# 128 rows instead of 64 for the mixer's small products, and products of one shape side by side

## The chip, the cores and the metric

The kernel runs on one core of a Trainium2 chip. Its engines work side by side, each through its own list of instructions in order: PE (TensorE) multiplies matrices, DVE (VectorE) and ACT (ScalarE) do elementwise work and reductions, POOL (GpSimd) does a little of that and issues some DMAs, SP issues most DMAs. Matrix products read SBUF and write PSUM. The metric is the device time of one execution in microseconds (us), lower is better. TensorE's clock has two levels here, 1.2 and 2.4 GHz; the profile shows the level as a granted share, 0.5 or 1.0.

## The reference

One layer of a streaming encoder over 256 tokens of width 2048, with 256 memory tokens. The residual x gets four updates, each wrapped in root-mean-square norms:

```python
x = x + 0.5 * post(FFN1(pre(x)))                  # SwiGLU, width 5504
x = x + post((gA * MLA(h) + gB * RWKV7(h)) @ w_o) # h = pre(x), the mixer
x = x + post(XAttn(pre(x), mem))                  # 4 heads of 256
x = x + 0.5 * post(FFN2(pre(x)))
```

The change lies in the mixer, in three places.

- MLA is attention with 8 heads. A head's score is a product over 128 columns without position plus one over 64 columns with a rotary position: `s = q_nope @ k_nope.T + q_rope @ k_r.T`. The rotary key `k_r` is one for all heads.
- RWKV7 makes its decay and its gate `a` by low-rank products: `tanh(dw) @ w_w2` and `da @ w_a2`, both with 64 inputs and 1024 outputs.
- RWKV7 then runs a recurrence over the tokens with a 64 x 64 state for each of 16 heads, `S = S * w + (S a) b^T + v k^T`, and reads `o = S r`.

## The kernel before

Activations are kept with features on the 128 partitions and tokens along the free axis, or the other way round. Weights stream from memory in tiles of 128 x 1024 numbers (512 KB): SP issues the load (`wraw`), ACT rounds it to fp32r (`whi`, line 179), DVE takes the rest (`wlo`, line 180), and PE does three products, high by high, low by high, high by low (lines 197 and 200 in `lin_ch`, 218 to 220 in `lin_tok`). These streams are most of the kernel's time.

The other products of the mixer are plain fp32 products. Each stands as two instructions in the trace (two passes), so four products show as x8. The profile gives the shape of the part of TensorE's array that an instruction uses: 128\*128 for 128 input rows by 128 output columns, 64\*128 for 64 input rows, 64\*64, 128\*64.

- `mla_attend` (line 568) has for each head and each of two query blocks a product with 128 rows (line 582) and one with 64 (line 583). Two heads share one tile of rotated queries `qrT`: the even head on partitions 0 to 63, the odd one on 64 to 127. The rotary key `krT` stands twice, once in each half. The query blocks have 128 and 256 key columns.
- `rw_prep` (line 692) prepares one group of 8 heads; it runs twice. At line 713 it has 4 low-rank products for the decay (rows 0 to 63 of `twa` and `ww`) and then 4 for `a` (rows 64 to 127), each over 256 tokens; ACT turns each into `lw` or `ta` (line 715). Line 720 scales `lw` once all four parts are there, and line 723 sums it along each chunk by a scan with a constant of zeros and ones that comes from memory in `cst`.
- `rw_gram` and `rw_inverse` then build and invert the within-chunk matrices. The inverse is a long row of small DVE instructions with a DMA to memory and back on both sides; PE goes on with `td` loaded back into `G`.
- `rw_chain` (line 841) walks 8 chunks of 32 tokens in order. In a chunk, for four pairs of heads: `po` gets state times inputs (line 848, 128\*128, not in the first chunk) and `G` times values (line 849, 64\*64); ACT copies `po` to `rhs`; PE multiplies by the inverse (line 856, 64\*64); DVE copies that to `uv`; PE makes the state's update `pn` (line 861, 128\*128) and the outputs (line 870, 128\*64); DVE makes the new state.

```python
for p in range(GP):
    if S is not None:
        nc.tensor.matmul(po[:, p, :], self.ar[:, c, p, :], S[:, p, :], ...)
    nc.tensor.matmul(po[:64, p, :], G[64:, c, p, :64], self.uv[64:, c, p, :], ...)
```

The order of each engine's list is fixed before the run by a planner that works with priorities: what stands in `hot()` (the low-rank products, the chain) comes first when its inputs are ready by the planner's reckoning, and the gaps are filled with products of less urgency: the projection of r and k during the attention, `out_a` and the gate products (`gate`, 8 blocks of columns) during the two groups. [...]

Of the kernel before, what the change touches and what calls it, by code (L numbers as in the profile page):

```python
# [10 lines left out]
F32 = mybir.dt.float32  # L11
F32R = mybir.dt.float32r
I32 = mybir.dt.int32
AF = mybir.ActivationFunctionType
ALU = mybir.AluOpType
# [3 lines left out]
P = 128  # L19
D = 2048  # L20
T = 256
# [29 lines left out]
CHUNK = 32  # L51
NC = T // CHUNK
GP = 4
HEADS_G = 2 * GP
# [2 lines left out]
TWO_PI_PARTS = (6.28125, 1.93500518798828125e-3, 2.0 * math.pi - 6.28125 - 1.93500518798828125e-3)  # L57
ROUND_MAGIC = 1.5 * 2.0 ** 23

CST = {"gram": 128, "sel": GP * HEADS_G, "scan": T}  # L60
NCST = sum(CST.values())


def _constants():
    out = {}
    row = np.arange(P)
    x, h, s = row // 64, row // 32 % 2, row % 32
    ok = np.where(x[None, :] == 0, s[:, None] < s[None, :], s[:, None] <= s[None, :])
    out["gram"] = (ok & (h[:, None] == h[None, :])).astype(np.float32)
    head = np.arange(GP)[None, :, None] + GP * (row[:, None, None] // 64)  # L70
    out["sel"] = (head == np.arange(HEADS_G)[None, None, :]).astype(np.float32).reshape(P, -1)
    out["scan"] = np.broadcast_to((np.arange(T) % CHUNK != 0).astype(np.float32), (P, T))
    m = np.zeros((P, 256), np.float32)
    m[:64, 192:] = -1.0e30
    inv = 10000.0 ** (-np.arange(32) / 32.0)
    return np.concatenate([out[n] for n in CST], axis=1), m, np.tile(inv.astype(np.float32), (P, 1))


class Layer:
# [416 lines left out]
    def mla_latents(self, mp, pool, normed):  # L496
        nc, w_in = self.nc, self.a["w_in"]
        h, r, _ = normed
        self.pad(pool, 224)
        self.cqh = pool.tile([P, 4, T], F32R, name="cqh")  # L500
        self.cql = pool.tile([P, 4, T], F32R, name="cql")
        self.ckh = pool.tile([P, 2, T], F32R, name="ckh")
        self.ckl = pool.tile([P, 2, T], F32R, name="ckl")
        self.krT = pool.tile([P, T], F32, name="krT")

        self.lin_tok(w_in, KD, 0, 512, h[:, :, 0], h[:, :, 1],
                     lambda t, ps: self.latent_norm(mp, ps, r, 512, self.cqh, self.cql, "n_q_lat", t))

        def ev(t, ps):
            self.latent_norm(mp, ps[:, :256], r, 256, self.ckh, self.ckl, "n_kv_lat", t)  # L510
            kr = pool.tile([P, 2, 2, 32], F32, tag="kr", name="kr", bufs=2)
            x1, x2 = ps[:, 256:288].unsqueeze(1), ps[:, 288:320].unsqueeze(1)
            self.rope(pool, x1, x2, kr[:, 0:1, 0, :], kr[:, 0:1, 1, :], t)
            nc.vector.tensor_scalar_mul(kr[:, 0], kr[:, 0], r[t])
            nc.vector.tensor_copy(out=kr[:, 1], in_=kr[:, 0])
            pt = self.pst.tile([P, P], F32, tag="tr", name="tr")
            nc.tensor.transpose(pt, kr.rearrange("p a b c -> p (a b c)"), self.ident)
            nc.scalar.copy(out=self.krT[:, t * P : (t + 1) * P], in_=pt)

        self.lin_tok(w_in, KD, 512, 320, h[:, :, 0], h[:, :, 1], ev)  # L520

# [46 lines left out]
    def mla_attend(self, pool):  # L568
        nc = self.nc
        oT = self.hpool.tile([P, 2, 8, T], F32R, tag="big", name="oT")  # L570
        self.oTh, self.oTl = oT[:, 0], oT[:, 1]
        mask = pool.tile([P, 256], F32, name="mask")
        nc.scalar.dma_start(out=mask, in_=self.a["mask"])
        scale = 192.0 ** -0.5
        for h in range(8):
            rp = slice(h % 2 * 64, h % 2 * 64 + 64)
            pt = self.pst.tile([P, 3, P], F32, tag="tr", name="tr")
            for qb in range(NT):
                n = (qb + 1) * P
                s = slice(qb * P, (qb + 1) * P)  # L580
                ps = self.pss.tile([P, 256], F32, tag="sm", name="sc")
                nc.tensor.matmul(ps[:, :n], self.qnT[:, h, s], self.knT[:, h, :n], start=True, stop=False)
                nc.tensor.matmul(ps[:, :n], self.qrT[rp, h // 2, s], self.krT[rp, :n], start=False, stop=True)
                sc = pool.tile([P, 256], F32, tag="sc", name="sc", bufs=2)
                nc.vector.tensor_add(sc[:, :n], ps[:, :n], mask[:, 256 - n :])
                p = self.softmax(pool, sc[:, :n], scale)
                for kb in range(qb + 1):
                    nc.tensor.transpose(pt[:, qb + kb, :], p[:, kb * P : (kb + 1) * P], self.ident)
            pT = pool.tile([P, 3, P], F32, tag="pT", name="pT", bufs=2)
            nc.scalar.copy(out=pT, in_=pt)  # L590
            po = self.pss.tile([P, T], F32, tag="sm", name="po")
            vs = slice(h * P, (h + 1) * P)
            nc.tensor.matmul(po, self.mv[:, 0, vs], pT[:, :2, :].rearrange("p a b -> p (a b)"), start=True, stop=False)
            nc.tensor.matmul(po[:, P:], self.mv[:, 1, vs], pT[:, 2, :], start=False, stop=True)
            self.split(po, self.oTh[:, h, :], self.oTl[:, h, :])
# [44 lines left out]
    def rw_proj_lora(self, pool, normed):  # L640
        h, _, row = normed
        nc = self.nc
        self.twa = pool.tile([P, T], F32, name="twa")
        self.sg = pool.tile([P, T], F32, name="sg")

        def ev(j, ps):
            dst, nm = ((self.twa, "wa"), (self.sg, "g"))[j]
            self.shifted(pool, dst, ps, row, self.col("mu_" + nm, 0), self.col2("omu_" + nm, 0))
            if j == 0:
                nc.scalar.activation(out=dst[:64], in_=dst[:64], func=AF.Tanh)  # L650
            else:
                nc.scalar.activation(out=dst, in_=dst, func=AF.Tanh, scale=0.5)
                nc.vector.tensor_scalar(out=dst, in0=dst, scalar1=0.5, scalar2=0.5, op0=ALU.mult, op1=ALU.add)

        self.lin_ch(self.a["w_in"], KD, 3904, 256, h, ev)
# [36 lines left out]
    def rw_prep(self, pool, g, r, k, bon):  # L692
        nc, a = self.nc, self.a
        p4 = lambda nm: pool.tile([P, GP, T], F32, tag="p4", name=nm, bufs=6)
        ww = pool.tile([P, 512], F32, tag="ww", name="ww")
# [3 lines left out]
        for h in range(2):  # L699
            o = g * 512 + h * 256  # L700
            nc.gpsimd.dma_start(
                out=self.uv[64 + h * 32 : 96 + h * 32].rearrange("s c p v -> s c (p v)"),
                in_=self.vsh[:, o : o + 256].rearrange("(c s) x -> s c x", s=CHUNK))
        nc.gpsimd.memset(self.bk, 0.0)

        lw, ta, kk = p4("lw"), p4("ta"), p4("kk")
        for dst, q, bias in ((lw, slice(0, 64), "hw0"), (ta, slice(64, P), "ha0")):
            for p2 in range(GP // 2):
                ps = self.pss.tile([P, 2, T], F32, tag="sm", name="lora")
                for j in range(2):  # L710
                    p = 2 * p2 + j
                    with self.hot():
                        nc.tensor.matmul(  # L713
                            ps[:, j, :], ww[q, p * P : (p + 1) * P], self.twa[q, :], start=True, stop=True)
                    nc.scalar.activation(
                        out=dst[:, p, :], in_=ps[:, j, :], func=AF.Tanh,
                        bias=self.col2(bias, g * GP + p), scale=0.5)
        for p in range(GP):
            nc.scalar.activation(out=kk[:, p, :], in_=k[:, p, :], func=AF.Copy, scale=self.col("k_k", g * GP + p))
        nc.vector.tensor_scalar(  # L720
            out=lw, in0=lw, scalar1=1.0, scalar2=-0.5 * KAPPA, op0=ALU.add, op1=ALU.mult)
        for p in range(GP):
            nc.vector.tensor_tensor_scan(
                out=lw[:, p, :], data0=self.c("scan"), data1=lw[:, p, :], initial=0.0, op0=ALU.mult, op1=ALU.add)
        sq = p4("sq")
        nc.scalar.activation(out=sq, in_=kk, func=AF.Square)
        sel = self.c("sel").rearrange("p (a b) -> p a b", a=GP)
        ssp = self.pss.tile([P, NT, HEADS_G], F32, tag="sm", name="ssp")
        for t in range(NT):
            for p in range(GP):  # L730
                with self.hot():
                    nc.tensor.matmul(
                        ssp[:, t, :], sq[:, p, t * P : (t + 1) * P], sel[:, p, :],
                        start=(p == 0), stop=(p == GP - 1))
# [3 lines left out]
            out=rt, in0=rt, in1=self.mhalf.unsqueeze(2).broadcast_to([P, NT, HEADS_G]), op=ALU.pow)  # L738
        x = pool.tile([P, NT, GP, P], F32, tag="p4", name="bych", bufs=6)
        for t in range(NT):  # L740
            for h in range(2):
                nc.vector.tensor_copy(
                    out=x[:, t, :, h * 64 : (h + 1) * 64],
                    in_=rt[:, t, h * GP : (h + 1) * GP].unsqueeze(2).broadcast_to([P, GP, 64]))
        for p2 in range(GP // 2):
            ps = self.pss.tile([P, 2, T], F32, tag="sm", name="rnb")
            for j in range(2):
# [5 lines left out]
                out=kk[:, 2 * p2 : 2 * p2 + 2, :], in0=kk[:, 2 * p2 : 2 * p2 + 2, :], scalar=-1.0, in1=ps,  # L753
# [87 lines left out]
    def rw_chain(self, pool, g, G, wc):  # L841
        nc = self.nc
        S = None
        for c in range(NC):
            po = self.pss.tile([P, GP, 64], F32, tag="sm", name="po")
            for p in range(GP):
                if S is not None:
                    nc.tensor.matmul(po[:, p, :], self.ar[:, c, p, :], S[:, p, :], start=(p == 0), stop=False)  # L848
                nc.tensor.matmul(  # L849
                    po[:64, p, :], G[64:, c, p, :64], self.uv[64:, c, p, :],  # L850
                    start=(S is None and p == 0), stop=(p == GP - 1))
# [353 lines left out]
```

## Time and profile before

| | us |
|---|---|
| median of 3 runs (lowest, highest) | 2438.91 (2430.94, 2445.75) |
| the profiled execution | 2441.6 |
| its span, first to last instruction | 2439.8 |

The page gives for each engine the time in which it was busy and, in 40 slices, how this changes. The mixer's attention lies at about 860 to 940 us of the span, the first group's preparation at 940 to 1075, its chain at 1075 to 1132, the second group's preparation at 1126 to 1265 and its chain at 1265 to 1332. In a timeline the first number is the start and the second the duration of an instruction or a merged row of them; passes overlap, so what a row takes from PE is read as the start of the next row less its own start.

### The profile page before, as it was taken

To read this page: it belongs to the slowest core of one execution; us is meant where nothing else is said; L and a number is where in the kernel's file an instruction comes from. 1 tells how busy PE (TensorE), PEld (TensorE's weight loads), DVE (VectorE), ACT (ScalarE), POOL (GpSimd) and SP (SyncE) were. 2 spreads that over 40 slices of the span, in tenths; PEclk is the share of its full clock that TensorE was granted. 3 is DMA by queue.
4 is the path that set the end of the run, shared out by engine and by line. 5 is a ranking of instruction groups with operands and counts; after the bars stand their busy time and mean duration, and the time that the engine had idled before them with its cause. 6 is when DMAs were issued, how large, how long until landed. Compare 5 with 4: busy or idle time off the path is not lost.

```text
span 2439.8 us, 33193 instructions
## 1 busy us (share of the span) xinstructions
PE 2385.9 (98%) x12682; PEld 2021.7 (83%) x12682; DVE 1487.9 (61%) x2262; ACT 1144.7 (47%) x1700; POOL 85.9 (4%) x126
## 2 busy tenths in 40 slices
PE   8999999999999999999999899999999999999997
PEld 6888888878878887887878688987888888888886
DVE  6666666644457576764873856555666666664444
ACT  6444444434446555443432446445544444444443
POOL 0000000000000102002011100000000000000000
PEclk9999999999999999998989999999999999999999
DMA  7555555556665643452553676545455555555654
GB/s 257 190 190 190 190 190 190 187 196 195 198 195 201 233 141 130 156 170 90 181 191 109 206 262 202 178 148 190 157 190 190 190 190 190 190 198 192 204 194 144
DMA packets 138719, 450.36 MB, mean 185 GB/s; under 512 B 24000, under 2 KB 26560, under 8 KB 138304
## 3 DMA queue, kind: packets, MB, share of 16 engines
q1 hardware_dynamic: 132896, 434.17, 53.1%
q0 software_dynamic: 4944, 13.64, 1.9%
q8 instruction: 99, 1.62, 0.3%
q10 hardware_dynamic: 720, 0.44, 0.1%
q14 instruction: 60, 0.49, 0.1%
HBM read 437.69 MB, written 10.49 MB: 184 GB/s over the span
## 4 chain that ended last, share of the span: by engine, by line
PE 91%; DVE 4%; DMA 2%; issue 1%; ACT 1%; POOL 1%; SPq 0%; DVEq 0%; ACTq 0%; POOLq 0%
PE mm L197 30%; PE mm L200 15%; PE mm L219 13%; PE mm L220 13%; PE mm L218 13%; DVE wlo L180 2%; PE po L848 1%; PE po L849 1%; PE gr L803 1%; PE pn L861 1%; ACT whi L179 1%; DMA ov<-osc 0%; PE lora L713 0%; PE po L870 0%; DVE X L387 0%
## 5 line engine op out<-in xcount | busy, mean ns | idle before, releaser
L180 DVE TENSOR_TENSOR wlo<-wraw,whi 128x1024 fp32r<-128x1024 f32 (+2 forms) x796 | 958.2, 1206 | 711.3 <-ACT whi L179 698.4
L179 ACT CAST whi<-wraw 128x1024 fp32r<-128x1024 f32 (+2 forms) x796 | 824.0, 1037 | 902.5 <-PE mm L220 484.2
L197 PE MATMUL mm<-hT,whi 128*128 128x512 f32 x3296 | 1146.9, 394 | 8.9 <-DVE hT L289 6.1
L200 PE MATMUL mm<-hT,wlo 128*128 128x256 f32 x3296 | 912.4, 282 | 1.9 <-DVE wlo L180 1.9
L197 PEld LDWEIGHTS mm<-hT,whi 128*128 128x128 f32 x3296 | 613.6, 188 | 137.8 <-ACT whi L179 7.1
L200 PEld LDWEIGHTS mm<-hT,wlo 128*128 128x128 f32 x3296 | 620.8, 188 | 15.5 <-DVE wlo L180 3.8
L218 PE MATMUL mm<-whi,mh 128*128 128x512 f32 x688 | 267.6, 389 | 1.2 <-ACT whi L179 1.2
L219 PE MATMUL mm<-wlo,mh 128*128 128x512 f32 x688 | 267.8, 389 | 0.5 <-DVE wlo L180 0.5
L220 PE MATMUL mm<-whi,ml 128*128 128x512 f32 x688 | 267.7, 389 | 0.0
L219 PE MATMUL mm<-wlo,hT 128*128 128x512 f32 (+2 forms) x512 | 190.8, 373 | 3.9 <-DVE wlo L180 3.9
L218 PE MATMUL mm<-whi,hT 128*128 128x512 f32 (+2 forms) x512 | 190.3, 373 | 1.9 <-ACT whi L179 1.7
L220 PE MATMUL mm<-whi,hT 128*128 128x512 f32 (+2 forms) x512 | 190.2, 372 | 0.0
L218 PEld LDWEIGHTS mm<-whi,mh 128*128 128x128 f32 x688 | 129.1, 188 | 28.1 <-ACT whi L179 1.5
L219 PEld LDWEIGHTS mm<-wlo,mh 128*128 128x128 f32 x688 | 129.2, 188 | 27.9 <-DVE wlo L180 1.0
L220 PEld LDWEIGHTS mm<-whi,ml 128*128 128x128 f32 x688 | 129.2, 188 | 26.7
L206 ACT COPY half<-mm 128x256 f32<-128x256 f32 x206 | 75.5, 367 | 137.6 <-PE mm L197 137.6
L207 DVE TENSOR_TENSOR half<-half,mm 128x256 f32<-128x256 f32 x206 | 85.6, 417 | 55.0 <-ACT half L206 55.0
L219 PEld LDWEIGHTS mm<-wlo,hT 128*128 128x128 f32 x512 | 99.2, 194 | 20.1 <-DVE wlo L180 5.2
L218 PEld LDWEIGHTS mm<-whi,hT 128*128 128x128 f32 x512 | 99.0, 194 | 17.7 <-ACT whi L179 2.3
L220 PEld LDWEIGHTS mm<-whi,hT 128*128 128x128 f32 x512 | 99.2, 194 | 15.5 <-issue 1.6
L252 POOL TENSOR_TENSOR rstd<-rstd,mhalf 128x1 f32<-128x1 f32 x22 | 12.0, 552 | 1812.5 <-DVE rstd L250 1798.7
L218 PE MATMUL mm<-whi,oT 128*128 128x512 f32 x128 | 51.4, 403 | 1.4 <-ACT whi L179 1.4
(276 smaller groups left out, 1896.5 us busy)
## 6 DMA issues: line engine op xcount, KB each, us to landing
wraw<-in_w_ffn_up SPq DMA_DIRECT2D x172, 512.0 KB, 4.3
wraw<-in_w_ffn_gate SPq DMA_DIRECT2D x171, 512.0 KB, 4.3
wraw<-in_w_ffn_down SPq DMA_DIRECT2D x168, 512.0 KB, 4.2
wraw<-in_w_in SPq DMA_DIRECT2D x124, 512.0 KB, 3.3
wraw<-in_w_o SPq DMA_DIRECT2D x32, 512.0 KB, 4.2
wraw<-in_w_ckv SPq DMA_DIRECT2D x31, 512.0 KB, 3.3
wraw<-in_w_oa SPq DMA_DIRECT2D x16, 512.0 KB, 3.2
wraw<-in_w_ob SPq DMA_DIRECT2D x16, 512.0 KB, 4.5
```

Source lines behind the costliest of these rows:

```text
L179: nc.scalar.copy(out=hi[:, e], in_=raw[:, e])
L180: self.last_split = nc.vector.tensor_sub(out=lo[:, e], in0=raw[:, e], in1=hi[:, e].bitcast(F32))
L197: both = lambda: nc.tensor.matmul(ps[j], hi[:, s], x[:, k], start=(k == 0), stop=(k == nk - 1))
L200: nc.tensor.matmul(ps[j][:, 0, :], lo[:, s], x[:, k, 0], start=False, stop=False)
L206: nc.scalar.copy(out=y, in_=ps[j][:, 1, :])
L207: nc.vector.tensor_add(y, y, ps[j][:, 0, :])
L218: nc.tensor.matmul(ps[t], xh[:, k, s], hi, start=(k == 0), stop=False)
L219: nc.tensor.matmul(ps[t], xh[:, k, s], lo, start=False, stop=False)
L220: self.last_mm = nc.tensor.matmul(ps[t], xl[:, k, s], hi, start=False, stop=(k == nk - 1))
L803: nc.tensor.matmul(ps[:, p, :], self.bk[:, c, p, :], self.ar[:, c, p, :], start=True, stop=True)
L848: nc.tensor.matmul(po[:, p, :], self.ar[:, c, p, :], S[:, p, :], start=(p == 0), stop=False)
L849: nc.tensor.matmul(po[:64, p, :], G[64:, c, p, :64], self.uv[64:, c, p, :], start=(S is None and p == 0), stop=(p == GP - 1))
```

## The change

The sums that are computed stay the same; zeros are added to operands, and one loop is cut in two.

- `krT` becomes two tiles side by side, one with the key in rows 0 to 63 and zeros below, one with zeros above. The product of line 583 then takes all 128 rows of `qrT`: the other head's queries meet zeros. POOL clears the tile, and ACT writes it with two copies for each token block instead of one.
- `twa` likewise becomes two: `tanh(dw)` with zeros below, `da` with zeros above, so that one product of 128 rows and 512 columns gives a decay part and an `a` part. Eight products for a group become four. The shifted projection is first written to `sg`, then moved.
- The scan's constant is not loaded but made by two POOL memsets in each group, in the buffer of `ww`, of which there is one: it waits until the low-rank products have read `ww`, and the load of `ww` for the second group waits for the scans of the first.
- In `rw_chain` all four products of line 848 come before the four of line 849.

```diff
-        self.krT = pool.tile([P, T], F32, name="krT")
+        self.krT = pool.tile([P, 2, T], F32, name="krT")
+        nc.gpsimd.memset(self.krT, 0.0)
...
-            nc.scalar.copy(out=self.krT[:, t * P : (t + 1) * P], in_=pt)
+            for j in range(2):
+                q = slice(j * 64, j * 64 + 64)
+                nc.scalar.copy(out=self.krT[q, j, t * P : (t + 1) * P], in_=pt[q])
...
-                nc.tensor.matmul(ps[:, :n], self.qrT[rp, h // 2, s], self.krT[rp, :n], start=False, stop=True)
+                nc.tensor.matmul(ps[:, :n], self.qrT[:, h // 2, s], self.krT[:, h % 2, :n], start=False, stop=True)
...
-        self.twa = pool.tile([P, T], F32, name="twa")
+        self.twa = pool.tile([P, 2, T], F32, name="twa")
+        nc.gpsimd.memset(self.twa, 0.0)
...
-                nc.scalar.activation(out=dst[:64], in_=dst[:64], func=AF.Tanh)
+                nc.scalar.activation(out=self.twa[:64, 0, :], in_=dst[:64], func=AF.Tanh)
+                nc.scalar.copy(out=self.twa[64:, 1, :], in_=dst[64:])
...
+        for p in range(GP):
+            ps = self.pss.tile([P, 2, T], F32, tag="sm", name="lora")
+            with self.hot():
+                nc.tensor.matmul(ps, ww[:, p * P : (p + 1) * P], self.twa, start=True, stop=True)
+            for j, (dst, bias) in enumerate(((lw, "hw0"), (ta, "ha0"))):
+                nc.scalar.activation(
+                    out=dst[:, p, :], in_=ps[:, j, :], func=AF.Tanh,
+                    bias=self.col2(bias, g * GP + p), scale=0.5)
+        scan = pool.tile([P, NC, CHUNK], F32, tag="ww", name="scan")
+        nc.gpsimd.memset(scan, 1.0)
+        nc.gpsimd.memset(scan[:, :, 0:1], 0.0)
...
             for p in range(GP):
                 if S is not None:
                     nc.tensor.matmul(po[:, p, :], self.ar[:, c, p, :], S[:, p, :], start=(p == 0), stop=False)
+            for p in range(GP):
                 nc.tensor.matmul(
                     po[:64, p, :], G[64:, c, p, :64], self.uv[64:, c, p, :],
```

## Rows read from the trace of the kernel before

**Rows 1.** The page's head, PE's line of part 1 (busy time, share of the span, instructions), and the granted clock in 40 slices of part 2 (tenths of full speed).

```profile
span 2439.8 us, 33193 instructions
PE 2385.9 (98%) x12682; PEld 2021.7 (83%) x12682; DVE 1487.9 (61%) x2262; ACT 1144.7 (47%) x1700; POOL 85.9 (4%) x126
PEclk9999999999999999998989999999999999999999
```

**Rows 2.** The chain that ended last, by engine, from part 4 of the page.

```profile
PE 91%; DVE 4%; DMA 2%; issue 1%; ACT 1%; POOL 1%; SPq 0%; DVEq 0%; ACTq 0%; POOLq 0%
```

**Rows 3.** Busy time by stretch: the stretch, its length, busy us and instructions of PE, PEld, DVE, ACT, POOL, then the granted clock, the DMA engines' share and GB/s. The latents, the attention, the first chain; then three stretches cut at the edges of a fall of the clock.

```profile
770.00:800.00 30.00, 28.68 (x153) 24.16 (x152) 18.88 (x43) 16.67 (x30) 2.75 (x5) 1.00 0.51 179
860.00:940.00 80.00, 78.02 (x412) 60.98 (x412) 54.72 (x151) 42.74 (x90) 4.96 (x4) 1.00 0.35 118
1075.00:1140.00 65.00, 65.00 (x389) 48.36 (x389) 23.09 (x38) 18.64 (x35) 12.61 (x19) 0.90 0.28 92
1123.80:1127.20 3.40, 3.40 (x21) 2.28 (x19) 0.00 (x0) 0.69 (x2) 2.66 (x3) 1.00 0.06 18
1127.20:1144.30 17.10, 17.10 (x51) 10.13 (x50) 4.68 (x7) 9.13 (x17) 2.20 (x4) 0.50 0.23 66
1263.70:1287.60 23.90, 23.27 (x86) 18.10 (x84) 9.73 (x16) 4.42 (x7) 3.79 (x5) 0.50 0.31 99
```

**Rows 4.** What PE waited for between 700 and 1420 us (line, releaser: us in total, times, longest); one row of it.

```profile
PE pu L856 <- DMA G<-td: 3.8, 1, 3.8
```

**Rows 5.** Timeline of PE in a chunk of the first chain: the first two of the eight alternating rows of lines 848 and 849, the gate products behind them, and the next chunk's first row.

```profile
1078.27 0.33 PE L848 MATMUL po<-S,ar 128*128 128x64 f32 x2
1078.54 0.33 PE L849 MATMUL po<-uv,G 64*64 64x64 f32 x2
...
1080.65 0.50 PE L220 MATMUL mm<-whi,hT 128*128 128x512 f32 x1
1080.99 0.39 PE L218 MATMUL mm<-whi,hT 128*128 128x512 f32 x1
1081.22 0.39 PE L219 MATMUL mm<-wlo,hT 128*128 128x512 f32 x1
...
1086.43 0.33 PE L848 MATMUL po<-S,ar 128*128 128x64 f32 x2
```

**Rows 6.** The same chunk's products that stand grouped by shape: four of 64\*64, and four of 128\*128 with 64 columns ahead of four of 128\*64.

```profile
1081.99 0.68 PE L856 MATMUL pu<-rhs,G 64*64 64x64 f32 x8
1082.60 0.50 PE L219 MATMUL mm<-wlo,hT 128*128 128x512 f32 x1
...
1083.63 1.00 PE L861 MATMUL pn<-uv,bk 128*128 128x64 f32 x8
1084.56 0.68 PE L870 MATMUL po<-uv,G 128*64 128x64 f32 x8
```

**Rows 7.** ACT in that chunk, the copy between lines 849 and 856 (in brackets the idle time before it and what ended it).

```profile
1080.76 0.37 ACT L853 COPY rhs<-po 64x256 f32<-64x256 f32 x1 [1.13 <-PE po L849]
```

**Rows 8.** The second chain's second chunk, at the granted clock 0.50: its first row and the gate product behind the eight; then the first row of the third chunk.

```profile
1272.37 0.52 PE L848 MATMUL po<-S,ar 128*128 128x64 f32 x2
...
1276.29 0.79 PE L219 MATMUL mm<-wlo,hT 128*128 128x512 f32 x1
...
1287.14 0.52 PE L848 MATMUL po<-S,ar 128*128 128x64 f32 x2
```

**Rows 9.** Timeline of PE in the attention, around one product of line 583.

```profile
875.65 0.39 PE L582 MATMUL sc<-knT,qnT 128*128 128x128 f32 x2
875.97 0.49 PE L583 MATMUL sc<-krT,qrT 64*128 64x128 f32 x2
876.38 0.50 PE L197 MATMUL mm<-hT,whi 128*128 128x512 f32 x1
876.72 0.28 PE L200 MATMUL mm<-hT,wlo 128*128 128x256 f32 x1
```

**Rows 10.** The low-rank products of the first group: a run of two products between products of `out_a`, and later a run of one.

```profile
944.84 1.13 PE L713 MATMUL lora<-twa,ww 64*128 64x256 f32 x4
945.90 0.51 PE L218 MATMUL mm<-whi,oT 128*128 128x512 f32 x1
946.33 1.13 PE L713 MATMUL lora<-twa,ww 64*128 64x256 f32 x4
...
947.82 0.70 PE L713 MATMUL lora<-twa,ww 64*128 64x256 f32 x2
948.45 0.49 PE L220 MATMUL mm<-whi,oT 128*128 128x512 f32 x1
```

**Rows 11.** The second group's, at the granted clock 0.50: a run of two products (a decay part and an `a` part) and a run of one.

```profile
1132.31 1.23 PE L713 MATMUL lora<-twa,ww 64*128 64x256 f32 x4
1133.47 0.80 PE L218 MATMUL mm<-whi,hT 128*128 128x512 f32 x1
1134.19 1.49 PE L713 MATMUL lora<-twa,ww 64*128 64x256 f32 x4
...
1136.33 1.22 PE L713 MATMUL lora<-twa,ww 64*128 64x256 f32 x2
1137.48 0.79 PE L220 MATMUL mm<-whi,hT 128*128 128x512 f32 x1
```

**Rows 12.** POOL clearing `bk` in the first group.

```profile
940.76 3.53 POOL L704 MEMSET bk<- 128x4096 f32 x1
```

More of the change, by code (lines that the diff above doesn't have):

```diff
@@ L58 @@
 ROUND_MAGIC = 1.5 * 2.0 ** 23
-CST = {"gram": 128, "sel": GP * HEADS_G, "scan": T}
+CST = {"gram": 128, "sel": GP * HEADS_G}
 NCST = sum(CST.values())
@@ L71, in _constants @@
     out["sel"] = (head == np.arange(HEADS_G)[None, None, :]).astype(np.float32).reshape(P, -1)
-    out["scan"] = np.broadcast_to((np.arange(T) % CHUNK != 0).astype(np.float32), (P, T))
     m = np.zeros((P, 256), np.float32)
@@ L575, in mla_attend @@
         for h in range(8):
-            rp = slice(h % 2 * 64, h % 2 * 64 + 64)
             pt = self.pst.tile([P, 3, P], F32, tag="tr", name="tr")
@@ L642, in rw_proj_lora @@
         nc = self.nc
-        self.twa = pool.tile([P, T], F32, name="twa")
+        self.twa = pool.tile([P, 2, T], F32, name="twa")
         self.sg = pool.tile([P, T], F32, name="sg")
+        nc.gpsimd.memset(self.twa, 0.0)
         def ev(j, ps):
-            dst, nm = ((self.twa, "wa"), (self.sg, "g"))[j]
+            dst, nm = self.sg, ("wa", "g")[j]
             self.shifted(pool, dst, ps, row, self.col("mu_" + nm, 0), self.col2("omu_" + nm, 0))
             if j == 0:
-                nc.scalar.activation(out=dst[:64], in_=dst[:64], func=AF.Tanh)
+                nc.scalar.activation(out=self.twa[:64, 0, :], in_=dst[:64], func=AF.Tanh)
+                nc.scalar.copy(out=self.twa[64:, 1, :], in_=dst[64:])
             else:
@@ L706, in rw_prep @@
         lw, ta, kk = p4("lw"), p4("ta"), p4("kk")
[L707 to L717, printed above, removed]
+        for p in range(GP):
[9 more added lines that the diff above has]
+        nc.gpsimd.memset(scan[:, :, 0:1], 0.0)
+        scan = scan.rearrange("q c s -> q (c s)")
         for p in range(GP):
@@ L723, in rw_prep @@
             nc.vector.tensor_tensor_scan(
-                out=lw[:, p, :], data0=self.c("scan"), data1=lw[:, p, :], initial=0.0, op0=ALU.mult, op1=ALU.add)
+                out=lw[:, p, :], data0=scan, data1=lw[:, p, :], initial=0.0, op0=ALU.mult, op1=ALU.add)
         sq = p4("sq")
```

## The prediction

> **What bounds the kernel now.** I read the page first: PE is busy for 98% of the span [rows 1], and the chain that ended last runs through PE for 91% of it [rows 2]. So PE bounds nearly everything, and time that leaves PE's list counts if nothing else becomes late. Then the stretches of the mixer: PE is busy for 78.02 of 80 us in the attention and for 65.00 of 65 in the first chain, where DVE has 23 and ACT 19 [rows 3]. The largest PE wait in the mixer for something other than weights or a norm is 3.8 us, once, for the inverse of the second group coming back by DMA [rows 4].
>
> A busy PE need not be a PE that gets on, so the third view is the timeline, read from start to start. In a chunk of the chain the gate products follow each other every 0.23 us (1080.99 to 1081.22), but the first one after the eight alternating products keeps PE for 0.34 (1080.65 to 1080.99) [rows 5]. The four pairs of lines 848 and 849 take 2.38 us (1078.27 to 1080.65). Products that stand grouped by shape are faster: four of 64\*64 take 0.61 (1081.99 to 1082.60), four of 128\*128 with 64 columns 0.93 (1083.63 to 1084.56), each with the step to the next shape in it [rows 6]. What costs is the step from one shape to another.
>
> The fourth is the clock. Its mean in the first chain's stretch is 0.90: from 1127.20 it is at 0.50 for 17.10 us, with PE busy for all of the 3.40 us before, in which lie the last alternating rows, one low-rank product and few gate products. It is at 0.50 again from 1263.70 for 23.90 us, behind the wait for the inverse [rows 3, 4].
>
> **The change, part by part.** The sum is made against the profiled execution, 2441.6 us (span 2439.8); the median of the runs shown is 2438.9, 2.7 less.
>
> *The chain's grouping.* Lines 848 and 849 keep their counts and shapes. Grouped, they should cost what lines 861 and 856 cost: 0.93 + 0.61 = 1.54 in place of 2.38, so 0.84 less a chunk [rows 5, 6]. The first chunk of a group has no line 848, so 2 x 7 = 14 chunks gain. One stands wholly at the lower clock and takes 3.92 (1272.37 to 1276.29) [rows 8]; its gain lies between 0.84 and the same share of 3.92, 1.38; I take 1.1. Together 13 x 0.84 + 1.1 = 12.0 us. Does a wait take its place? ACT's copy to `rhs` starts at 1080.76, just behind the last 64\*64 product, ends at 1081.13, and line 856 starts at 1081.99 [rows 6, 7]: 0.86 us of slack, filled by gate products, and the change moves the end of line 849 and the copy together.
>
> *The attention's rotary product.* Two passes of 256 columns differ by 0.43 (below), so two of 128 need 0.22. Line 582 ahead of line 583 takes 0.32 (875.65 to 875.97), line 583 itself 0.41, and the weight product behind it 0.34 in place of 0.23 [rows 5, 9]: 0.10 + 0.19 + 0.11 = 0.40 us for one step out and back. All of it goes, since the product with zeros has the shape of its neighbours and the same columns. 16 products give 6.4 us. A gain as small as half of this would need DVE or ACT to set the pace there; they are busy for 55 and 43 of 80 us [rows 3].
>
> *The low-rank products, first group.* A run of two products takes 1.06 (944.84 to 945.90), a run of one 0.63 (947.82 to 948.45): one product is 0.43, and 0.20 of each run is the step. The single weight product between two runs takes 0.43 in place of 0.23 (945.90 to 946.33), so 0.20 more [rows 5, 10]. That is again 0.40 for each run, and 5 runs give 2.0 us. The columns stay: 4 products of 512 columns, 0.86 each as twice 0.43, against 8 of 0.43.
>
> *The second group* has six runs, one at the full clock and five at the lower one. There a run of one takes 1.15 (1136.33 to 1137.48) and a run of two 1.16 (1132.31 to 1133.47): a decay part on rows 0 to 63 and an `a` part on rows 64 to 127 ran at the same time [rows 11]. So the runs hold about 0.63 + 3 x 1.15 + 1.16 + 1.49 = 6.7 us, and four products of 512 columns at that clock would hold 4 x 1.72 = 6.9: no gain inside. The weight product between two runs takes 0.72 (1133.47 to 1134.19) against some 0.45, twice the 0.23 of the full clock, so about 0.3 more [rows 5, 11]; over five runs 5 x 0.3 = 1.5, with the loss of 0.2 and the first run's 0.1 some 1.4 us.
>
> The Trainium skill has a rule that speaks against this part: TensorE: Matmul & The Clock Gate, Part 3 (Packing small matmuls), says that products of few rows in different row groups run at the same time. The trace agrees where the planner happened to put two such side by side [rows 11], and in the first group, where each run held two decay parts or two `a` parts, it shows none [rows 10]. By that rule the eight products of a group, paired, would need 4 x 0.43 instead of the 4 x 0.86 with zeros: 1.7 us a group, or 3.4 in all, that the zeros give away against a packed version, though not against this kernel.
>
> *The clock.* The fall at 1127.20 came behind the place where most steps lay together. With the chain grouped and the low-rank product in the neighbours' shape that place is denser. If the fall stays away, the 17.10 us need about half, so up to 8.5 less, of which 1.4 is counted already: 7 more. If it comes as before, nothing. I take half, 3.5: it comes, but is over sooner, since the five runs within it no longer break the stream.
>
> *What is added.* POOL clears `krT` and `twa` (512 columns each) and makes the scan's constant twice (256 and 8): at 3.53 us for 4096 columns [rows 12] some 1.3 us in all, on an engine that is busy for 86 us of the span [rows 1]. In the second group `lw` is complete after the seventh tanh instead of the fourth, and the scan waits for POOL; what it feeds is needed after the key's norm has gone through PE, POOL and DVE, and PE has gate products meanwhile. I cost it at nothing; without that cover it would be two products and a memset, 2 x 0.86 + 0.23, or 2 us a group. ACT gets three copies of 64 partitions more, 0.37 each by the nearest row [rows 7], two of them in the latents' stretch, where PE lacks 1.3 of 30 us [rows 3]: between 0 and 1.1; I take 1.1, as this is the one place where ACT could be late. POOL's load of the second `ww` now stands behind the first group's scans, long before that group's products use it.
>
> Sum: 12.0 + 6.4 + 2.0 + 1.4 + 3.5 - 1.1 = 24.2 us. 2441.6 - 24.2 = 2417.4; against the median 2438.9 it is 2414.7. I forecast 2415.
>
> **Rivals.**
> - *The clock no longer falls in the chains.* For it: the fall at 1127.20 had no idle PE ahead of it, only steps. Against: the second one stands behind the wait for the inverse, which the change doesn't touch. Both gone would give up to 3.5 + 12 (half of 23.90) more; with the first gone and the second shortened by half, 2415 - 3.5 - 6 = about 2405, at the far end 2400. Chance 0.17.
> - *The gain becomes a wait for the inverse.* PE already waits 3.8 us there [rows 4]; DVE's row of small instructions sets that time. What is saved before the second group's low-rank products moves DVE's start as well, what is saved in and after them (1.4 + 3.5) does not: 2415 + 5 = 2420. If the attention's and the first group's gains (8.4) were held up as well, 2428. Chance 0.14.
> - *The change does not do what it says:* the planner's order changes with the fewer low-rank products, gate products land between the chain's products, and the chain keeps its steps. Then only 6.4 + 2.0 + 1.4 remain, 2429. Against: the chain's instructions are urgent and all ready at once. Chance 0.05.
> - *Slower: the chain runs at the lower clock.* A chunk takes 8.16 us at the full clock (1078.27 to 1086.43) and 14.77 at the lower one (1272.37 to 1287.14) [rows 5, 8], so 6.6 more. Shorter urgent rows could leave PE waiting between them, and a wait stood ahead of the second fall. The gain of 24 is used up from the fourth further chunk; from the sixth the kernel is over 0.5% slower. With seven, one whole chain, 2415 + 46 = 2461. Against: with less dense work the clock was at 0.50 for only two pieces of the chains [rows 3], and each hand-over is filled. Chance 0.06.
>
> **How the numbers follow.** The forecast has 0.58, with its own range 2408 to 2422. Faster by over 0.5%, about what a measurement of this kernel can tell from no change, means under 2426.7: the forecast, the first rival and about half of the second, 0.82. The rest of the second and the third are within 0.5%: 0.12. Slower 0.06. The range reaches from the first rival's 2400 to past the third's 2429, 2432.
>
> **What would show it.** Lines 583 and 713 as 128\*128; the step from 64\*64 to 128\*128 ahead of line 848 gone, and line 848's first row to the end of line 849 taking 1.5 us instead of 2.4; weight products behind lines 583 and 713 at 0.23 us. PE's busy time about 20 us less, with its instructions down by 16. Wrong it would be if 1.5 us show and the span doesn't shrink by 20: then PE's waits, above all for `G<-td`, have grown, or the clock's row shows longer stretches at 0.50.

## The result, and the profile after

The changed kernel takes 2409.56 us (median of 4 runs, 2409.18 to 2411.64) against 2434.93 for the kernel before, run 4 times (2430.35 to 2445.75): ratio 0.9891, 95% interval 0.9854 to 0.9928, 25.4 us less. The forecast was 2415, some 24 less, in a range from 2400 to 2432. The profiled executions are 30.0 us apart, 2441.6 and 2411.64; that of before lay well above its median, at a mean granted clock of 0.986 against 0.992.

The page's head, PE's line and the granted clock of the changed kernel, then its chain by engine, as [rows 1, 2]:

```profile
span 2409.9 us, 33179 instructions
PE 2355.2 (98%) x12666; PEld 2006.5 (83%) x12666; DVE 1487.8 (62%) x2262; ACT 1145.7 (48%) x1703; POOL 87.8 (4%) x132
PEclk9999999999999999999999999999999999999999
PE 90%; DMA 3%; DVE 3%; issue 2%; ACT 1%; POOL 1%; SPq 0%; DVEq 0%; POOLq 0%; ACTq 0%
```

PE's busy time fell by 30.7 us and the span by 29.9, and PE has 16 instructions fewer. DVE, ACT and POOL are busy for the same time as before to within 2 us: nothing but PE's list got shorter, and PE still bounds the kernel. A part of the 30.7 is the clock's: the two eights in its row of [rows 1] are gone.

PE in the first chunk of the first chain that has a state, in the changed kernel (line 849 is now 854, line 856 is 861):

```profile
1074.63 1.00 PE L852 MATMUL po<-S,ar 128*128 128x64 f32 x8
1075.56 0.67 PE L854 MATMUL po<-uv,G 64*64 64x64 f32 x8
1076.16 0.50 PE L219 MATMUL mm<-whi,hT 128*128 128x512 f32 x1
1076.50 0.39 PE L217 MATMUL mm<-whi,hT 128*128 128x512 f32 x1
...
1077.51 0.67 PE L861 MATMUL pu<-rhs,G 64*64 64x64 f32 x8
...
1081.94 1.00 PE L852 MATMUL po<-S,ar 128*128 128x64 f32 x8
```

From 1074.63 to 1076.16 the eight products take 1.53 us, against 2.38 in [rows 5]. The next chunk starts 7.31 later, against 8.16, so the whole 0.85 reaches the chunk's period; line 861 starts 1.35 behind the first gate product (1076.16 to 1077.51), against 1.34 before, without a wait.

The attention, as [rows 9], and the low-rank products of the second group, as [rows 11]:

```profile
876.97 0.39 PE L583 MATMUL sc<-knT,qnT 128*128 128x128 f32 x2
877.19 0.39 PE L584 MATMUL sc<-krT,qrT 128*128 128x128 f32 x2
877.33 0.48 PE L196 MATMUL mm<-hT,whi 128*128 128x512 f32 x1
877.65 0.28 PE L199 MATMUL mm<-hT,wlo 128*128 128x256 f32 x1
...
1118.88 1.02 PE L713 MATMUL lora<-twa,ww 128*128 128x512 f32 x2
1119.83 0.68 PE L875 MATMUL po<-uv,G 128*64 128x64 f32 x8
...
1121.24 1.88 PE L713 MATMUL lora<-twa,ww 128*128 128x512 f32 x4
1122.56 0.80 PE L218 MATMUL mm<-wlo,hT 128*128 128x512 f32 x1
1123.19 0.39 PE L219 MATMUL mm<-whi,hT 128*128 128x512 f32 x1
```

The product ahead of the rotary one (line 582 before, 583 here) takes 0.22 in place of 0.32. From its start to that of the second weight product it is 0.68 us, where [rows 9] have 1.07 (875.65 to 876.72): 0.39 less, one step out and back. Two of the wide low-rank products and the gate product behind them take 1.95 us (1121.24 to 1123.19), which is 2 x 0.86 and 0.23 with no step; one ahead of a 128\*64 row takes 0.95 (1118.88 to 1119.83), so there 0.09 of a step is left.

Five stretches of the changed kernel, columns as in [rows 3]: the attention, the end of the first chain with the low-rank products, the fall of the clock in the second chain, and two short falls, one over the first group's low-rank products and one behind the mixer:

```profile
860.00:940.00 80.00, 76.60 (x433) 64.25 (x432) 58.31 (x162) 44.94 (x94) 8.62 (x6) 1.00 0.43 135
1116.60:1127.60 11.00, 11.00 (x60) 7.32 (x58) 4.77 (x7) 8.96 (x18) 3.84 (x9) 1.00 0.29 82
1244.40:1254.70 10.30, 9.32 (x37) 7.28 (x36) 7.02 (x13) 2.04 (x3) 2.41 (x3) 0.50 0.61 206
940.70:944.10 3.40, 3.30 (x5) 1.51 (x5) 0.00 (x0) 1.21 (x3) 0.00 (x0) 0.51 1.02 265
1483.40:1486.80 3.40, 3.40 (x17) 3.40 (x18) 3.40 (x8) 2.62 (x8) 0.00 (x0) 0.50 0.89 289
```

Two of PE's waits between 700 and 1400 us, as [rows 4]:

```profile
PE pu L861 <- DMA G<-td: 3.3, 1, 3.3
PE lora L713 <- DMA ww<-in_w_a: 2.2, 1, 2.2
```

The stretch that ran at the clock 0.50 for 17.10 us [rows 3] runs at 1.00. The second fall, behind the wait for the inverse, is still there, 10.3 us long in place of 23.90. The wait for the inverse did not grow (3.8 in [rows 4]); a wait for the first group's low-rank weights is new.

### The profile page after: what moved, and what is told of

Its sections match the earlier page's. It is cut to its first block, busy times and chain, and to the rows that moved or that the text cites. A ratio compares the mean times of both kernels' runs of the same rounds, so it can differ in the third digit from the quotient of the medians.

```text
span 2409.9 us, 33179 instructions
## 1 busy us (share of the span) xinstructions
PE 2355.2 (98%) x12666; PEld 2006.5 (83%) x12666; DVE 1487.8 (62%) x2262; ACT 1145.7 (48%) x1703; POOL 87.8 (4%) x132
## 4 chain that ended last, share of the span: by engine, by line
PE 90%; DMA 3%; DVE 3%; issue 2%; ACT 1%; POOL 1%; SPq 0%; DVEq 0%; POOLq 0%; ACTq 0%
PE mm L196 30%; PE mm L199 16%; PE mm L218 13%; PE mm L219 13%; PE mm L217 13%; DVE wlo L179 1%; DMA ov<-osc 1%; PE gr L807 1%; ACT whi L178 1%; DMA wraw<-in_xT 1%; PE pn L866 1%; DVE X L386 1%; PE po L852 0%; PE po L875 0%; PE po L854 0%
## 5 line engine op out<-in xcount | busy, mean ns | idle before, releaser
L217 PE MATMUL mm<-whi,hT 128*128 128x512 f32 (+2 forms) x512 | 187.3, 367 | 2.1 <-ACT whi L178 1.5
L219 PE MATMUL mm<-whi,hT 128*128 128x512 f32 (+2 forms) x512 | 187.9, 368 | 0.0
L206 DVE TENSOR_TENSOR half<-half,mm 128x256 f32<-128x256 f32 x206 | 85.7, 418 | 54.8 <-ACT half L205 54.8
```

Of the source, the lines that this page charges most:

```text
L206: nc.vector.tensor_add(y, y, ps[j][:, 0, :])
L217: nc.tensor.matmul(ps[t], xh[:, k, s], hi, start=(k == 0), stop=False)
L219: self.last_mm = nc.tensor.matmul(ps[t], xl[:, k, s], hi, start=False, stop=(k == nk - 1))
```

## The experiments

The runs of the kernel before scatter over more than 20 us, and with them their mean granted clock, from 0.983 to 0.993. Over the 46 runs of it beside the experiments, a straight line gives 2.0 us for each 0.001 of clock. So each kernel is shown by its median and also by the mean of its runs at 0.992 and 0.993, which compares the work at nearly one clock (called the equal clock below); and by how many runs lay under 0.990. Where a kernel was run twice, its runs are taken together. The runs beside the experiments come from three chips; at the equal clock the kernel before took 2428.5, 2429.3 and 2429.0 us on them. The scatter of the runs leaves a standard error of 0.4 to 1.1 us on each of these means, so a difference of one or two us between them is not clear of noise.

| kernel | medians, us | runs | under 0.990 | at 0.992 and 0.993 (runs) |
|---|---|---|---|---|
| before | 2432.0, 2437.1, 2432.3 | 46 | 16 | 2428.8 (20) |
| grouping alone | 2416.6, 2415.0 | 12 | 0 | 2416.3 (10) |
| rotary product alone | 2426.3 | 12 | 2 | 2423.2 (4) |
| low-rank products alone | 2425.3 | 12 | 2 | 2425.0 (8) |
| all but the grouping | 2417.7, 2419.6 | 12 | 0 | 2419.6 (8) |
| the changed kernel | 2409.6, 2408.1 | 10 | 0 | 2409.5 (7) |
| more alternation | 2419.0 | 7 | 1 | 2419.4 (5) |
| packed low-rank products | 2415.0 | 6 | 0 | 2411.7 (2) |
| low-rank weights first | 2407.9 | 6 | 0 | 2407.2 (2) |

**One part at a time.** Grouping alone is the last piece of the diff put into the kernel before:

```diff
...
                     nc.tensor.matmul(po[:, p, :], self.ar[:, c, p, :], S[:, p, :], start=(p == 0), stop=False)
+            for p in range(GP):
                 nc.tensor.matmul(
...
```

> The kernel before with the grouping of lines 848 and 849 alone. Theory (the price is in the steps between shapes, the clock follows from how dense the work is): the eight products of a chunk take 1.54 us in place of 2.38, 14 chunks give 12 us less; the second clock fall (23.9 us before, 10.2 after) is short here too, which gives up to 6 more; the fall at the end of the first chain may stay, as the low-rank runs are as before. 2417 to 2425. Rival (the low-rank products' steps make both falls): 12 us less and both falls as long as before.

Measured: 2416.59, ratio to the kernel before 0.9924 (0.9900 to 0.9947), just under the range expected; at the equal clock 12.5 us less, against 12.0 by the steps. In its profile the second fall was 10.2 us long and the one at the end of the first chain did not come, though the low-rank runs were as before.

The rotary product alone takes the edits of `krT` and line 583:

```diff
...
-                nc.tensor.matmul(ps[:, :n], self.qrT[rp, h // 2, s], self.krT[rp, :n], start=False, stop=True)
+                nc.tensor.matmul(ps[:, :n], self.qrT[:, h // 2, s], self.krT[:, h % 2, :n], start=False, stop=True)
...
```

> The kernel before with the 128-row rotary product alone. Theory: 16 steps out and back at 0.40 us, 6.4 us less in the attention, of which a part becomes a wait for the first group's low-rank weights behind it: 3 to 6 us less. Rival (the attention is paced by ACT and DVE): under 2 us less, with PE's waits in the attention longer. Clock falls in the chains as before in both.

Measured: 2426.27, ratio 0.9966 (0.9945 to 0.9987), 5.7 us less at the equal clock. In its profile the first to the last score product span 60.6 us, where the kernel before has 66.0, and PE is busy for all of it in both. The steps were the price, and behind the attention one wait is new: the low-rank products waited 1.1 us for their weights,

```profile
PE lora L715 <- DMA ww<-in_w_w: 1.1, 1, 1.1
```

a row that the kernel before does not have. The attention is not paced by ACT or DVE. The falls did not stay "as before": in this profile they lasted 3.4 us at the end of the first chain and 3.4 in the second, with one of 10.2 over the first group's low-rank products.

The low-rank products alone take the edits of `twa`, the product and the scan's constant:

```diff
...
-        for dst, q, bias in ((lw, slice(0, 64), "hw0"), (ta, slice(64, P), "ha0")):
...
+        for p in range(GP):
+            ps = self.pss.tile([P, 2, T], F32, tag="sm", name="lora")
+            with self.hot():
+                nc.tensor.matmul(ps, ww[:, p * P : (p + 1) * P], self.twa, start=True, stop=True)
...
```

> The kernel before with the 128-row low-rank products, and the scan's constant made by POOL, alone. Theory: steps alone give 2.0 us in the first group and 1.4 to 3 in the second; the fall at the end of the first chain stays, since the alternating products ahead of it are as before: 3 to 5 us less. Rival (the low-rank runs make that fall): it is gone, 8 to 11 us less.

Measured: 2425.26, ratio 0.9969 (0.9951 to 0.9988), 3.8 us less at the equal clock, against 2.0 + 1.4 by the steps. In its profiled execution the fall at the end of the first chain was gone, with the chain alternating as before, so the part of the theory that hung the fall on the alternation fell. The 8 to 11 us of the rival did not come either. But its runs at 0.989 take 2433 and 2434: low clocks still occur.

**The grouping undone** in the changed kernel:

```diff
...
-            for p in range(GP):
                 nc.tensor.matmul(
                     po[:64, p, :], G[64:, c, p, :64], self.uv[64:, c, p, :],
...
```

> The changed kernel with lines 848 and 849 alternating again. Theory: 12 us more than the changed kernel by steps, and up to 6 more as the second clock fall is long again: 2421 to 2428. Rival (the falls hang on the low-rank products): 12 us more, and the second fall stays at 10 us.

Measured: 2417.69, ratio to the kernel before 0.9931 (0.9908 to 0.9955), under the range expected. At the equal clock that is 10.1 us over the changed kernel, a little under the 12 of the steps. In the chains themselves the 12 are there: from the first to the last product with the inverse its profile has 53.4 and 60.6 us in the two groups, that of the changed kernel 47.5 and 54.8, together 11.7. Outside the chains the two short falls of the changed kernel, at 940.70 and 1483.40, have no counterpart here; a second profile of the changed kernel has both. Its second fall was 10.2 us long, as in the changed kernel: the theory's "long again" was wrong. In this profile the alternating chain by itself does not bring the clock down:

```profile
1067.00:1120.00 53.00, 53.00 (x359) 42.00 (x358) 19.25 (x31) 12.56 (x22) 10.35 (x15) 1.00 0.29 100
```

This is the first chain of that kernel, all at 1.00.

**The clock, by more runs.** The changed kernel again, then grouping alone and all but the grouping again:

> The changed kernel once more, beside the runs of before and the three below on one chip. Theory: at an equal granted clock it is 18 to 22 us below before, and its runs spread less in clock (0.991 to 0.993) than those of before (0.983 to 0.993). Rival (the clock's spread has nothing to do with the change): runs under 0.990 turn up here about as often as before, 7 of 23.

> Grouping alone once more, for its clock. Theory (the low clock in some runs needs the alternating chain and the low-rank products' steps together): no run under 0.990, as in the first six; about 12 us under before at an equal clock. Rival (the low-rank products' steps alone can bring it): some runs under 0.990, as with before.

> All but the grouping once more, for its clock. Theory (it needs both together): no run under 0.990, as in the first six; about 10 us over the changed kernel. Rival (the alternating chain alone brings it): two or more of the runs under 0.990.

Measured: 2408.11 (ratio 0.9894, 0.9874 to 0.9914), 2415.04 (0.9928, 0.9913 to 0.9944) and 2419.60 (0.9948, 0.9929 to 0.9967). On one chip, beside each other, the changed kernel takes 20.3 us less than the kernel before at the equal clock, within the 18 to 22 expected. None of these 18 runs lay under 0.990. Together 0 of 34 runs of these three kernels did, against 16 of 46 before, so the change does steady the clock. Which part does it stays open: grouping alone was enough, the two other parts together were enough without it, and each of these two alone left 2 of 12. "It needs both together" is in line with this, but so is that every step less makes a low clock rarer.

**The step priced by itself.** In the changed kernel the state's update and the outputs, which stood grouped all along, alternate:

```diff
...
+            for p in range(GP):
+                if c < NC - 1:
+                    nc.tensor.matmul(pn[:, p, :], self.bk[:, c, p, :], self.uv[:, c, p, :], start=True, stop=True)
+                nc.tensor.matmul(
+                    po[64:, p, :], G[:, c, p, 64:], self.uv[:, c, p, :],
+                    start=(S is None and p == 0), stop=(p == GP - 1))
...
```

> The changed kernel with lines 866 and 875 (state update 128*128, outputs 128*64) alternating pair by pair as 848 and 849 did before. Theory: a step costs the same between these two shapes: eight products take 2.4 us in place of 1.54, 14 chunks give 12 us more, up to 16 if the new state then comes late for the next chunk. Rival (the price belonged to the 64-row products): under 4 us more.

Measured: 2419.02, 10.9 us over the changed kernel beside it, 9.9 at the equal clock, so a little under the 12 to 16 expected; in the two chains of its profile it is 11.6 (53.5 and 60.4 us, against 47.5 and 54.8). The timeline of PE has the pattern of [rows 5], now with shapes that all have 128 rows:

```profile
1075.00 0.33 PE L867 MATMUL pn<-uv,bk 128*128 128x64 f32 x2
1075.26 0.33 PE L868 MATMUL po<-uv,G 128*64 128x64 f32 x2
1075.52 0.43 PE L867 MATMUL pn<-uv,bk 128*128 128x64 f32 x2
...
1077.39 0.50 PE L219 MATMUL mm<-whi,hT 128*128 128x512 f32 x1
```

Eight products take 2.39 us (1075.00 to 1077.39), where the same eight grouped take 1.54 (0.93 and 0.61 in [rows 6], 1079.14 to 1080.68 in the changed kernel). A change of the columns alone costs here what the change of rows and columns cost in [rows 5], 0.85 us for three more steps out and back, so 0.28 for each; the price is not one of the 64-row products.

**Packing instead of zeros.** In the changed kernel the low-rank products stay at 64 rows, a decay part and an `a` part always side by side:

```diff
...
+            pl = [self.pss.tile([P, 2, T], F32, tag="sm", name="lora") for _ in range(2)]
+            for j in range(2):
+                p = 2 * p2 + j
+                for i in range(2):
+                    q = slice(i * 64, i * 64 + 64)
+                    with self.hot():
+                        nc.tensor.matmul(
+                            pl[i][:, j, :], ww[q, p * P : (p + 1) * P], self.twa[q, i, :], start=True, stop=True)
...
```

> The changed kernel with the low-rank products as 64-row products again, but a decay part and an a part always side by side on different rows and in different PSUM buffers. Theory (two of them run at once): a run of four products takes 1.26 us with its steps, 2.5 for a group in place of 3.4 with zeros, so 1 to 2 us less in all, within what the runs can tell; the timeline shows it. Rival (they run one after the other at the full clock): 1.06 us for two, 0.8 us more in all.

Measured: 2415.02, 6.9 us over the changed kernel beside it, where one to two us less was expected. The two do run at once,

```profile
1125.28 1.46 PE L717 MATMUL lora<-twa,ww 64*128 64x256 f32 x8
1126.68 0.50 PE L217 MATMUL mm<-whi,hT 128*128 128x512 f32 x1
```

four products in 1.40 us with the step out, where one after the other they need 4 x 0.43 and the step. But half of the products in each group were broken up. In the first group two decay parts were out before the `a` part's weights had come:

```profile
939.40 1.10 PE L717 MATMUL lora<-twa,ww 64*128 64x256 f32 x4 [0.70 <-DMA ww<-in_w_w]
941.15 1.72 PE L717 MATMUL lora<-twa,ww 64*128 64x256 f32 x4 [0.65 <-DMA ww<-in_w_a]
```

and in the second the chain's hurried products came in between, each time a step. Its runs lay at lower clocks (0.990 to 0.992), and most of the 6.9 is the clock's: its two runs at 0.992 average 2411.7 us, the changed kernel's four at that clock 2411.0. So packing shows no gain over the zeros, and no clear loss. The rule of the Trainium skill (TensorE: Matmul & The Clock Gate, Part 3, Packing small matmuls), that small products in different parts of the array run at the same time, held here, with four in 1.40 us; that this pays here was not seen.

**The new wait.** POOL issues the loads of `ww` ahead of clearing `ar`:

```diff
-        self.nc.gpsimd.memset(self.ar, 0.0)
...
+        if g == 0:
+            nc.gpsimd.memset(self.ar, 0.0)
         nc.gpsimd.memset(self.bk, 0.0)
```

> The changed kernel with POOL issuing the loads of the first group's low-rank weights ahead of clearing the array ar, not behind it. Theory: PE's wait of 2.2 us for these weights, in which part of the attention's gain was lost, goes: 2 to 3 us less. Rival (PE has other work then, or something else is late): nothing.

Measured: 2407.85, 0.3 us under the changed kernel beside it, where two to three were expected: no change that can be told. The wait is still there,

```profile
PE lora L714 <- DMA ww<-in_w_a: 2.0, 1, 2.0
```

because the planner put the products earlier too: they start at 934.86 in this profile, 10.1 us behind the last score product, where the changed kernel has 14.3. A part of this lead went in the products themselves, which ran under a fall of 6.8 us here and of 3.4 there. The rest was lost on DVE and POOL: one of the two memsets of the scan's constant stood on POOL behind the key's norm, and the scans behind it delayed the copies that PE's next urgent products need. The timeline of POOL,

```profile
950.42 0.11 POOL L721 MEMSET scan<- 128x8 f32 x1
```

and on DVE

```profile
950.68 1.85 DVE L728 TENSOR_TENSOR_SCAN lw<-scan,lw 128x256 f32<-128x256 f32 x3
954.16 0.67 DVE L747 COPY bych<-rt 128x256 f32<-128x256 f32 x3
```

The products that read these copies start 29.9 us behind the last score product here and 29.8 in the changed kernel, so the lead was gone by then. That the memset is the reason is read from this order; no run moved it. The constant made on POOL, which I costed at nothing, showed no cost when the low-rank products were changed alone; here it is one of the things that are late next.

## Why the prediction was right

- *What bounds the kernel, and the step as the price.* Right, and shown by itself: undoing the grouping, and alternating two other products, each cost some 10 us in the runs, and 11.7 and 11.6 in the chains of their profiles; in the timeline a chunk's eight products take 0.85 us more. The third rival, a chain that keeps its steps, is out by the same rows.
- *The chain, 12.0 us.* Grouping alone measured 12.5 at the equal clock, and the chains of the profiles 11.7. No wait took its place: line 861 follows as before.
- *The attention, 6.4.* Alone it measured 5.7, and 5.4 between the first and the last score product. The sign named for it, a weight product of 0.23 behind line 583, does not show by itself: that one takes 0.32 (877.33 to 877.65), and the rotary product ahead of it 0.14 in place of the 0.22 reckoned. Their sum is the one expected.
- *The low-rank products, 2.0 + 1.4.* Alone they measured 3.8.
- *The sum.* The steps' 21.8 less 1.1 for ACT's copies made 20.7; the changed kernel measured 19.3 at the equal clock. The parts alone add up to 22.0, so no run shows the 1.1, and 2.7 less came out together than apart, with a standard error of some 1.8. The second rival put such a loss at the inverse; that wait did not grow. The profiles put about half of it at the first group's low-rank products. From the last score product to the first product with the inverse in that group the kernel before takes 144.3 us, the low-rank products alone 142.8, and the changed kernel in its two profiles 144.2 and 144.0, each with one fall of 3.4 us on the way. So the 1.5 gained there alone is all but gone, and PE's wait for the weights stands in that stretch: 0.4 with the low-rank products alone, 2.2 and 1.9 in the changed kernel. That the wait makes the loss was not shown, as the run meant to take it away did not.
- *The clock, 3.5.* Here the mechanism was only half right. I had one profiled execution and read its two falls as the kernel's. They were that run's: its mean clock was 0.986, only 5 of the 46 runs of before are as low, and a third lie under 0.990; no other profile has a fall longer than 10.3 us in the chains. So what the clock is worth depends on the runs compared. The medians of the result are 25.4 us apart and the work at the equal clock 19.3, so there it is about 6 us, between the forecast and the first rival, which named it; by the medians of all the runs in the table (2432.5 and 2409.2) it is 4; between the two profiled executions it is 11 (30.0 less 19.3). That the total came so near the sum, 25.4 against 24.2, is partly luck: the work was 1.4 less than reckoned and the clock 2.6 more. The last forecast step, that the fall comes but is over sooner, describes the second fall of the profiles (10.3 us in place of 23.90), not the first, which did not come.
- *The slower rival*, more chunks at the lower clock: none of the runs of the changed kernel was under 0.991.

## What to carry to other kernels

Read the timeline of a busy TensorE from start to start, and by shape: here a step to another shape in rows or columns and back cost 0.40 us amid full products and 0.28 in the chain's small ones, so products of one shape belong side by side, and a narrow product amid full ones was cheaper with zeros than by itself. Before a term is made of the clock in one profile, see whether the runs differ among themselves; comparing runs at one granted clock separates the work from it.

## What the runs showed that I had not expected

The mean granted clock of one kernel, alone on its core, ran from 0.983 to 0.993, and 0.001 of it was worth 2.0 us of some 2430. Fewer steps between shapes made the low values disappear (0 of 34 runs in three kernels against 16 of 46). And two products of 64 rows side by side ran at once at the full clock too, yet the kernel that relied on this was no faster than the one that fills the rows with zeros (2411.7 against 2411.0 at the clock 0.992).
